# Block products by Strassen's scheme in the second product of two MLPs of a float32 encoder

## The chip, the cores and the metric

One core of a Trainium2 chip runs the whole kernel. The metric is the device time of one execution in microseconds; of several runs the median counts.

## The reference

Four layers with residual adds on x (256 tokens, 1024 features, float32): an attention layer, an MLP, a second attention layer (dilated windows), an MLP, and a last RMSNorm. The change is in the MLPs:

```
def sq_relu_mlp(xn, w1, w2):
    return jnp.square(jax.nn.relu(xn @ w1)) @ w2
...
    x = x + sq_relu_mlp(rms_norm(x, norm_mlp[layer]), mlp_w1[layer], mlp_w2[layer])
```

w1 is 1024 x 4096, w2 is 4096 x 1024.

## The kernel before

Every product is computed with operands split in two: hi (a cast on ScalarE, ACT) and lo (the value less hi, a subtraction on VectorE, DVE), and `mm3` (L170) issues three matmuls, hi by hi, hi by lo and lo by hi. So each weight tile passes through a fixed path. `load_weight` (L129) has SyncE's queue (SP) load a raw tile of 128 x 2048 (1 MB) into one of four buffers; `split_piece` (L144) splits it in four pieces of 512 into whi (L167) and wlo (L168); `weight` (L158) hands it to TensorE (PE) and, before that, loads up to four tiles and splits up to two tiles ahead. The order of the tiles stands in the list `specs`; `plan_mlp` (L104) writes an MLP's part of it: up 0, up 1, up 2, down 0, up 3, down 1 and so on to down 15. Each engine works its queue in order; the scheduler sorts the instructions into it when the program is built, and a block under `tc.high_priority` goes earlier.

An MLP (`mlp`, L308) has 16 steps over 256 hidden features each. `up(j)` (L313) computes two blocks of 128 hidden features for the 256 tokens, 48 matmuls with 256 columns, into one PSUM bank `w`; then relu on ACT (L325), its product with itself `hsq` on DVE (L327), and the split into hh and hl. `down(j)` multiplies the hidden blocks by the w2 tile: two blocks of tokens t, two blocks of hidden features f, two halves of the output features h, that is 2 x 2 x 2 = 8 block products of three matmuls with 512 columns, `mm_down` (L345), all summed in four PSUM banks `acc`, one for each t and h. PE's order is up 0, up 1, up 2, down 0, up 3, down 1 and so on.

`hand_over` (L262) precedes each MLP: from the banks of the layer before, DVE adds into x (L270), two blocks at a time, and `prepare` (L204) makes xh on ACT (L207) and xl on DVE (L208); up 0 takes them in that order, k = 0 to 3 first. The squares of x for the norm follow on DVE (L215, L217).

The first MLP ends in `turn_over` (L360): the last two steps are done bank by bank, and each finished bank is scaled by ACT into y (L390), transposed by PE (L372), added into x by DVE (L374) and made into xh and xl for the next layer, while PE goes on with the next bank; the fourth bank is turned behind the first value products of the next layer. The second MLP ends in `finish` (L394): x has been transposed to tokens first between the steps; each bank is scaled and added by DVE in one instruction (`residual`, L425), the last bank in two parts, then its squares are summed (L455), POOL (GpSimd) raises the sum to the power -1/2 (L198), and ACT and DVE scale the last two blocks, which go out on two queues.

Of the kernel before, what the change touches and what calls it, by code (L numbers as in the profile page):

```python
# [44 lines left out]
def trunk(ctx, tc, a, out):  # L46
# [97 lines left out]
    def split_piece(eng=None):  # L144
        j, i = divmod(state["split"], WPARTS)
        if i == 0:
            parts[j][1:] = (wsp.tile([P, WCH], F32R, tag=n, name=n) for n in ("whi", "wlo"))
        raw, hi, lo = (z[:, cut(j, i, WPARTS)] for z in parts[j])
        state["split"] += 1
        return split(hi, lo, raw, eng)  # L150
# [900 lines left out]
```

## Time and profile before

| | us |
|---|---|
| median of 3 runs | 755.83 (755.81 to 755.87) |
| the profiled execution, its own time | 755.33 |
| its span | 753.6 |
| PE busy | 746.0 (99%) |
| DVE busy | 503.5 (67%) |
| ACT busy | 503.0 (67%) |
| POOL busy | 8.3 (1%) |
| bytes moved by DMA | 129.08 MB, mean 171 GB/s |

The profile is one execution; its lines name the engine, the line of the kernel (L168), the operation and the tiles as out<-in. A matmul's row gives its start and a duration that overlaps with the next one; the distance between two starts is what one costs. "Idle before" is the time in which the engine waited, with what released it.

### The profile page before, as it was taken

Reading aid. Unit: us, or ns where it says so; the run is one execution under the profiler, and the core shown is the slowest. Engines: PE = TensorE matmul, PEld = TensorE weight load, DVE = VectorE, ACT = ScalarE, POOL = GpSimd, SP = SyncE. Lnnn points to the kernel's source line nnn. Section 1 sums busy time; section 2 is a strip of 40 time slices with the busy share of each in tenths; the row PEclk is TensorE's granted clock in tenths of the full one; section 3 lists DMA queues with packets and bytes.
Section 4 is the critical chain, followed back from the end, with each engine's and each line's share of the span. In section 5 each row is a group of like instructions: output and inputs, shape, how many; then the busy total and the mean of one; then the engine's idle time right before and its main releaser. Section 6 shows DMA issues by size and latency. Waiting matters only on the chain.

```text
span 753.6 us, 13848 instructions
## 1 busy us (share of the span) xinstructions
PE 746.0 (99%) x5532; PEld 697.1 (93%) x5532; DVE 503.5 (67%) x1035; ACT 503.0 (67%) x1068; POOL 8.3 (1%) x19
## 2 busy tenths in 40 slices
PE   9999999999999999999999999999999999999996
PEld 6998999899899898999999999999999999899895
DVE  6878858555555556886777677677768554555564
ACT  7778867554554546988988989889856544544541
POOL 0100000000000001000000000000000000000000
PEclk9999999999999999999999999999999999999999
DMA  8772324555455544544453444444553545455501
GB/s 316 278 266 99 114 112 168 177 215 175 180 204 178 187 167 150 209 152 141 168 161 142 159 166 171 156 140 168 205 216 135 195 174 197 173 190 183 187 22 56
DMA packets 22383, 129.08 MB, mean 171 GB/s; under 512 B 2864, under 2 KB 4400, under 8 KB 9648
## 3 DMA queue, kind: packets, MB, share of 16 engines
q1 hardware_dynamic: 22032, 127.94, 47.8%
q8 instruction: 43, 0.70, 0.4%
q10 hardware_dynamic: 288, 0.28, 0.1%
q14 instruction: 20, 0.16, 0.1%
HBM read 127.16 MB, written 1.05 MB: 170 GB/s over the span
## 4 chain that ended last, share of the span: by engine, by line
PE 97%; ACT 1%; issue 1%; DVE 0%; POOLq 0%; POOL 0%
PE acc L171 21%; PE acc L172 20%; PE acc L173 20%; PE w L171 9%; PE w L173 9%; PE w L172 9%; PE w L180 1%; PE w L899 1%; PE w L716 1%; PE w L881 1%; PE acc L914 1%; PE w L730 1%; PE w L622 1%; PE acc L82 0%; PE acc L730 0%
## 5 line engine op out<-in xcount | busy, mean ns | idle before, releaser
L168 DVE TENSOR_TENSOR wlo<-raw,whi 128x512 fp32r<-128x512 f32 (+3 forms) x488 | 307.5, 664 | 168.9 <-ACT whi L167 168.4
L167 ACT CAST whi<-raw 128x512 fp32r<-128x512 f32 (+3 forms) x488 | 268.6, 600 | 190.8 <-issue 167.1
L173 PE MATMUL w<-xh,wlo 128*128 128x256 f32 x528 | 149.4, 283 | 0.0
L172 PE MATMUL w<-xl,whi 128*128 128x256 f32 x528 | 149.4, 283 | 0.0
L171 PE MATMUL w<-xh,whi 128*128 128x256 f32 x528 | 149.4, 283 | 0.0
L171 PE MATMUL acc<-xh,whi 128*128 128x256 f32 x432 | 125.4, 290 | 0.0
L173 PE MATMUL acc<-xh,wlo 128*128 128x256 f32 x432 | 122.3, 283 | 0.0
L172 PE MATMUL acc<-xl,whi 128*128 128x256 f32 x432 | 122.1, 283 | 0.0
L171 PEld LDWEIGHTS w<-xh,whi 128*128 128x128 f32 x528 | 101.3, 192 | 1.1
L172 PEld LDWEIGHTS w<-xl,whi 128*128 128x128 f32 x528 | 101.3, 192 | 1.1
L173 PEld LDWEIGHTS w<-xh,wlo 128*128 128x128 f32 x528 | 101.3, 192 | 0.0
L171 PE MATMUL acc<-whi,hh 128*128 128x512 f32 x250 | 98.1, 392 | 0.0
L172 PE MATMUL acc<-wlo,hh 128*128 128x512 f32 x250 | 97.8, 391 | 0.0
L173 PE MATMUL acc<-whi,hl 128*128 128x512 f32 x250 | 97.5, 390 | 0.0
L171 PEld LDWEIGHTS acc<-xh,whi 128*128 128x128 f32 x432 | 82.6, 191 | 1.3 <-issue 0.3
L172 PEld LDWEIGHTS acc<-xl,whi 128*128 128x128 f32 x432 | 82.7, 191 | 0.0
L173 PEld LDWEIGHTS acc<-xh,wlo 128*128 128x128 f32 x432 | 82.6, 191 | 0.0
L171 PE MATMUL acc<-whi,xh 128*128 128x384 f32 (+2 forms) x160 | 56.0, 350 | 0.0
L173 PEld LDWEIGHTS acc<-whi,hl 128*128 128x128 f32 x250 | 46.9, 188 | 9.8
L171 PEld LDWEIGHTS acc<-whi,hh 128*128 128x128 f32 x250 | 47.0, 188 | 9.1
L172 PEld LDWEIGHTS acc<-wlo,hh 128*128 128x128 f32 x250 | 47.1, 188 | 8.8
L172 PE MATMUL acc<-wlo,xh 128*128 128x384 f32 (+2 forms) x160 | 55.2, 345 | 0.0
(197 smaller groups left out, 1085.1 us busy)
## 6 DMA issues: line engine op xcount, KB each, us to landing
raw<-in_w SPq DMA_DIRECT2D x64, 1024.0 KB, 4.8
raw<-in_w_oqk SPq DMA_DIRECT2D x24, 1024.0 KB, 4.8
raw<-in_w_ov SPq DMA_DIRECT2D x16, 768.0 KB, 4.3
raw<-in_w_oe SPq DMA_DIRECT2D x4, 1024.0 KB, 5.3
raw<-in_w_oo SPq DMA_DIRECT2D x4, 1024.0 KB, 4.8
raw<-in_w_qk SPq DMA_DIRECT2D x3, 1024.0 KB, 9.1
raw<-in_w_cv SPq DMA_DIRECT2D x6, 464.0 KB, 7.8
bias<-in_rpb SPq DMA_DIRECT2D x8, 256.0 KB, 3.4
```

Of the source, the lines that this page charges most:

```text
L167: a = nc.scalar.copy(hi, src).ins
L168: return a, (eng or nc.vector).tensor_tensor(lo, src, hi.bitcast(F32), op=ALU.subtract).ins
L171: nc.tensor.matmul(o, sh, mh, start=first, stop=False)
L172: nc.tensor.matmul(o, sh, ml, start=False, stop=False)
L173: nc.tensor.matmul(o, sl, mh, start=False, stop=last)
L180: nc.tensor.matmul(o[j], y[pb, 0, ts], z[pb, 1, :], start=n == 0, stop=n == 2)
L622: nc.tensor.transpose(pt[0:96, i * P:(i + 1) * P], src[:, i, :], ident)
L716: nc.tensor.transpose(pt[:, b * P:(b + 1) * P], pp[:, b // 2, (b % 2) * P:(b % 2 + 1) * P], ident)
L730: nc.tensor.matmul(pvo[64 * j:64 * j + 64, 0:P], v[:, kk, h * 64:(h + 1) * 64], pts[:, 2 * j + kk, :], start=kk == 0, stop=kk == NT - 1)
L881: nc.tensor.matmul(ss[i, j][rows, T:T + P], d["q12"][:, j, i * P + 64 * c:i * P + 64 * c + 64], d["k12"][:, j, 2 * i + c, :], start=True, ...
L899: nc.tensor.transpose(pt[:, b * P:(b + 1) * P], pp[:, b * P:(b + 1) * P], ident)
L914: nc.tensor.matmul(pvo[cs, tok(i)], d["v0"][:, kk, cs], pts[j][:, kk, :], start=kk == 0, stop=False)
```

## The change

Of each step's second product, the 2 x 2 blocks of hidden values (t by f) and the 2 x 2 blocks of the w2 tile (f by h) are multiplied by seven products in place of eight. Four products (P1, P2, Q3, Q5 on the weight side) take a block as stored or one sum, three take larger sums; each of the seven has a PSUM bank of its own through the whole MLP, so that all eight banks are in use with the one of `up`. The outputs are combined from the seven banks once, at the end of the MLP.

For that:

- The w2 tile is stored as blocks b11, b21, b22, b12. SP loads the 1 MB as before and b12 (256 KB) a second time, into the tile `sum`. Two accumulating transfers from POOL's queue add b11 onto the fourth block of the raw tile and b22 onto the first of `sum`. DVE makes two more sums of 512 columns (`more_sums`, L174 and L175; called S1 and S2 below), and the three blocks of `sum` are split like weights, in one piece of 1536 (sumh, suml). Tiles of `sum`, sumh and suml have two buffers.
- The pieces of all MLP weights' splits are 1024 columns in place of 512.
- Hidden values: relu and the square on ACT, three differences on DVE (L367 to L369), and one split of seven blocks, 896 columns (hh, hl).
- `turn_over` combines the seven banks by instructions of DVE (L400), each a bank times a token's scale (one over the mean square of x) plus or minus a tile; four groups of transposes use the bank of `up`. Two of the four turns (`late`) are done between the next layer's value products, whose order is changed.
- `finish` combines likewise; the 16 transposes of x stand behind the last `up`, and the last product, Q4, is made in two parts of 256 columns.

The lines of the changed kernel are other ones: splits are L196 and L197, the sums into x L299, xh and xl L236 and L237, the sum of the turned block into x L419.

```diff
-        for j in (0, 1):
-            specs.append((a["w1"][layer, j], WCH))
-        for j in range(2, 16):
-            specs.append((a["w1"][layer, j], WCH))
-            specs.append((a["w2"][layer, j - 2], WCH))
-        for j in (14, 15):
-            specs.append((a["w2"][layer, j], WCH))
+        up = [(a["w1"][layer, j], WCH, 2, False) for j in range(16)]
+        down = [(a["w2"][layer, j], WCH, 2, True) for j in range(16)]
+        specs.extend(up[:3])
+        for j in range(13):
+            specs.extend((down[j], up[j + 3]))
+        specs.extend(down[13:])
...
+        if blocks:
+
+            b11, b22, b12 = (src[:, b * BLK:(b + 1) * BLK] for b in (0, 2, 3))
+            sums = state["pool"].tile([P, 3, BLK], F32, tag="sum", name="sum", bufs=2)
+            nc.sync.dma_start(sums[:, 0, :], b12)
+            nc.gpsimd.dma_start(raw[:, 3 * BLK:], b11, accum_op=ALU.add)
+            nc.gpsimd.dma_start(sums[:, 0, :], b22, accum_op=ALU.add)
+            parts[j].append(sums)
...
+                more_sums(*parts[j])
+        if i == n:
+            parts[j][4:] = (state["pool"].tile([P, 3, BLK], F32R, tag=n, name=n, bufs=2) for n in ("sumh", "suml"))
...
+    def more_sums(raw, hi, lo, sums):
+
+        nc.vector.tensor_tensor(sums[:, 1, :], sums[:, 0, :], raw[:, 0:BLK], op=ALU.add)
+        nc.vector.tensor_tensor(sums[:, 2, :], sums[:, 1, :], raw[:, BLK:2 * BLK], op=ALU.add)
...
+    HID = {"Q3": 0, "Q6": 1, "Q5": 2, "Q7": 3, "P2": 4, "Q4": 5, "P1": 6}
+
+
+    COL = {"P1": 0, "P2": 1, "Q3": 2, "Q5": 3, "Q7": 4, "Q6": 5, "Q4": 6}
+    PRODUCTS = ("P1", "P2", "Q5", "Q7", "Q3", "Q6", "Q4")
...
-                        mm3(pu[:, f * T:(f + 1) * T], w[0][:, c], w[1][:, c], xT[0][:, k, :], xT[1][:, k, :],
+                        mm3(pu[:, (1 - f) * T:(2 - f) * T], w[0][:, c], w[1][:, c], xT[0][:, k, :], xT[1][:, k, :],
                             k == 0 and (f == 0 or j > 0), k == KT - 1 and (f == 1 or j > 0))
             r = scratch([512], "relu")
             nc.scalar.activation(r, pu, AF.Relu)
-            h = scratch([512], "hsq")
-            nc.vector.tensor_tensor(h, r, pu, op=ALU.mult)
-            hs[j] = tuple(mp.tile([P, 512], F32R, tag=n, name=n, bufs=4) for n in ("hh", "hl"))
-            split(*hs[j], h)
+            h = mp.tile([P, 8, P], F32, tag="h", name="h", bufs=1)
+            nc.scalar.activation(h[:, 4:8, :], r.rearrange("p (b n) -> p b n", n=P), AF.Square)
+            nc.vector.tensor_tensor(h[:, 2:4, :], h[:, 7:8, :].broadcast_to([P, 2, P]), h[:, 5:7, :], op=ALU.subtract)
+            nc.vector.tensor_tensor(h[:, 1, :], h[:, 6, :], h[:, 2, :], op=ALU.subtract)
+            nc.vector.tensor_tensor(h[:, 0, :], h[:, 4, :], h[:, 1, :], op=ALU.subtract)
+            hh = act.tile([P, KT // 2, T], F32R, tag="quarter", name="hh", bufs=4).rearrange("p a (b n) -> p (a b) n", n=P)
+            hl = mp.tile([P, 7, P], F32R, tag="hl", name="hl", bufs=3)
+            hs[j] = hh, hl
+            split(hh[:, 0:7, :], hl, h[:, 0:7, :])
+
+        def down(j, w, o, n, first, last, c=slice(0, BLK)):
+            i, b = HID[n], COL[n]
+            mm3(o, hs[j][0][:, i, :], hs[j][1][:, i, :], w[0][b][:, c], w[1][b][:, c], first, last)
...
+        m = {n: bank("w" if i < 3 else "acc") for i, n in enumerate(("P1", "P2", "Q6", "Q3", "Q5", "Q7", "Q4"))}
+        pu = bank("w")
+        for j in range(14):
+            if j:
+                up(j + 2, pu)
             w = weight()
-            for f in range(2):
-                down(j, w, f)
-            if j + 3 < 16:
-                up(j + 3)
-            beside(j)
-        return accs, hs, inv, {j: weight() for j in tail}
-
-    def mm_down(acc, hs, j, w, f, t, c0, c1, first, last):
-
-        tk, c = slice(f * T + t * P, f * T + (t + 1) * P), slice(f * D + c0, f * D + c1)
-        mm3(acc, hs[j][0][:, tk], hs[j][1][:, tk], w[0][:, c], w[1][:, c], first, last)
+            for n in PRODUCTS:
+                down(j, w, m[n], n, j == 0, j == 13 and n in apart)
...
+    def onto_tokens(o, m, scale, v, op=ALU.add):
+
+        nc.vector.scalar_tensor_tensor(o, m, scale, v, ALU.mult, op)
...
+        sc = lambda: scratch([512], "y")
+        last("P1")
+        with tc.high_priority(NORM_PRIO):
+            p0, p1 = sc(), sc()
+            nc.scalar.activation(p0, m["P1"], AF.Copy, scale=i0)
+            nc.scalar.activation(p1, m["P1"], AF.Copy, scale=i1)
+        last("P2")
+        y[0, 0] = step(sc(), "P2", i0, p0)
+        last("Q6")
+        v0 = step(sc(), "Q6", i0, p0, ALU.subtract)
+        turn(0, 0)
+        last("Q5")
+        v0 = step(sc(), "Q5", i0, v0)
+        last("Q3")
+        y[0, 1] = step(sc(), "Q3", i0, v0)
+        v1 = step(sc(), "Q6", i1, p1, ALU.subtract)
+        last("Q7")
+        v1 = step(sc(), "Q7", i1, v1)
+        y[1, 1] = step(sc(), "Q5", i1, v1)
+        turn(0, 1)
+        last("Q4")
+        y[1, 0] = step(sc(), "Q4", i1, v1, ALU.subtract)
+        return xT, s, [lambda: turn(1, 1), lambda: turn(1, 0)]
...
+        last("Q3")
+        onto_tokens(v[0, 1], m["Q3"], i0, v[0, 1])
         ss = work.tile([P, 4], F32, tag="ssf", name="ss")
+        for h in range(2):
+            square_sum(v[0, h], ss[:, h:h + 1])
+        w1 = scratch([512], "w1")
+        onto_tokens(w1, m["Q6"], i1, p1, ALU.subtract)
+        onto_tokens(v[1, 1], m["Q5"], i1, v[1, 1])
+        last("Q7")
         nc.vector.tensor_scalar(ss[:, 2:3], ss[:, 0:1], ss[:, 1:2], EPS, ALU.add, ALU.add)
         r = rsqrt(ss[:, 2:3], "x")
         for h, cs in enumerate(HALF):
             y = scratch([512], "y")
+            nc.vector.scalar_tensor_tensor(y, v[0, h], r, g[h], ALU.mult, ALU.mult)
             nc.sync.dma_start(out[0:P, cs], y)
 
 
         ss = work.tile([P, 4], F32, tag="ssf", name="ss")
         xg = [scratch([512], "xg") for _ in range(2)]
...
+        for i, c in enumerate((slice(0, 256), slice(256, 512))):
+            o = bank("w")[:, 0:256]
+            last("Q4", o, c)
+            z = v[1, 0][:, c]
+            onto_tokens(z, o, i1, z)
+            if i == 0:
+                square_sum(z, ss[:, 1:2])
...
-        v0[0]()
-        late()
-        run_all(v0[1:])
+
+        run_all([late[0], v0[0], late[1], v0[1], v0[3], v0[2]])
```

The steady step on DVE. Before, one step of the first MLP (raw, whi, wlo: weights; hsq, hl: hidden values):

```order
L168 TENSOR_TENSOR wlo<-raw,whi 128x512 [waits DMAHW0_49,PE_49,Activation_49]
L327 TENSOR_TENSOR hsq<-relu,w 128x512 [waits Activation_49]
L168 TENSOR_TENSOR wlo<-raw,whi 128x512 [waits Activation_49] x2
L168 TENSOR_TENSOR hl<-hsq,hh 128x512 [waits Activation_49]
L168 TENSOR_TENSOR wlo<-raw,whi 128x512 [waits Activation_49]
L168 TENSOR_TENSOR wlo<-raw,whi 128x512 [waits DMAHW1_49,Activation_49]
L168 TENSOR_TENSOR wlo<-raw,whi 128x512 [waits Activation_49] x3
```

After, one step of it:

```order
L174 TENSOR_TENSOR sum<-sum,raw 128x512 [waits DMAHW4_49,DMASW6_49]
L175 TENSOR_TENSOR sum<-sum,raw 128x512 [waits DVE_49]
L197 TENSOR_TENSOR wlo<-raw,whi 128x1024 [waits PE_49,Activation_49]
L197 TENSOR_TENSOR wlo<-raw,whi 128x1024 [waits DMASW5_49,Activation_49]
L367 TENSOR_TENSOR h<-h 128x256 [waits Activation_49]
L368 TENSOR_TENSOR h<-h 128x128 [waits DVE_49]
L369 TENSOR_TENSOR h<-h 128x128 [waits DVE_49]
L197 TENSOR_TENSOR wlo<-raw,whi 128x1024 [waits DMAHW2_49,Activation_49]
L197 TENSOR_TENSOR wlo<-raw,whi 128x1024 [waits Activation_49]
L197 TENSOR_TENSOR hl<-h,hh 128x896 [waits Activation_49]
L197 TENSOR_TENSOR suml<-sum,sumh 128x1536 [waits Activation_49]
```

Nine subtractions and one product, all of 512, have become eleven instructions of other sizes, and the two sums S1 and S2 (L174, L175), which wait for transfers of SP and of POOL's queue (DMAHW, DMASW), stand between the split of the three sums and the splits of the tile that is due next.

The entry of the second MLP on DVE. Before, from the first sum into x:

```order
L270 TENSOR_TENSOR x<-acc,x 128x512 [waits PE_49] x2
L208 SCALAR_TENSOR_TENSOR xl<-x,gains,xh 128x256 [waits Activation_49] x4
L270 TENSOR_TENSOR x<-acc,x 128x512 [waits PE_49] x2
L168 TENSOR_TENSOR wlo<-raw,whi 128x512 [waits DMAHW0_49,Activation_49]
L208 SCALAR_TENSOR_TENSOR xl<-x,gains,xh 128x256 [waits Activation_49] x4
L215 TENSOR_TENSOR squares<-squares,q 128x512
L215 TENSOR_TENSOR squares<-squares,q 128x512 [waits DVE_49,Activation_49]
```

After, the same place:

```order
L299 TENSOR_TENSOR x<-acc,x 128x512 [waits PE_49] x2
L237 SCALAR_TENSOR_TENSOR xl<-x,gains,xh 128x256 [waits Activation_49] x4
L299 TENSOR_TENSOR x<-acc,x 128x512 [waits PE_49] x2
L174 TENSOR_TENSOR sum<-sum,raw 128x512 [waits DMAHW1_49,DMASW1_49]
L197 TENSOR_TENSOR wlo<-raw,whi 128x1024 [waits DMAHW0_49,Activation_49]
L237 SCALAR_TENSOR_TENSOR xl<-x,gains,xh 128x256 [waits Activation_49] x4
L244 TENSOR_TENSOR squares<-squares,q 128x512
L197 TENSOR_TENSOR wlo<-raw,whi 128x1024 [waits Activation_49]
L244 TENSOR_TENSOR squares<-squares,q 128x512 [waits DVE_49]
L175 TENSOR_TENSOR sum<-sum,raw 128x512
```

Between the second pair of sums into x and the second four xl, where one split of 512 stood, there are now S1 of the first down tile, with its waits for two transfers, and a split of 1024.

The end of the first MLP on DVE. Before, from the first sum of a turned block into x (y is combined output, xl and wlo belong to the next layer):

```order
L374 TENSOR_TENSOR x<-w,x 128x4x128 [waits PE_49]
L208 SCALAR_TENSOR_TENSOR xl<-x,gains,xh 128x128 [waits Activation_49] x4
L374 TENSOR_TENSOR x<-w,x 128x4x128 [waits PE_49]
L208 SCALAR_TENSOR_TENSOR xl<-x,gains,xh 128x128 [waits Activation_49] x4
L374 TENSOR_TENSOR x<-w,x 128x4x128 [waits PE_49]
L168 TENSOR_TENSOR wlo<-raw,whi 128x384 [waits DMAHW0_49,Activation_49]
L208 SCALAR_TENSOR_TENSOR xl<-x,gains,xh 128x128 [waits Activation_49] x4
L168 TENSOR_TENSOR wlo<-raw,whi 128x384 [waits Activation_49]
L374 TENSOR_TENSOR x<-w,x 128x4x128 [waits PE_49]
L168 TENSOR_TENSOR wlo<-raw,whi 128x384 [waits Activation_49] x2
L208 SCALAR_TENSOR_TENSOR xl<-x,gains,xh 128x128 [waits Activation_49] x4
```

After, from the first combination:

```order
L400 SCALAR_TENSOR_TENSOR y<-w,ms,y 128x512 [waits PE_49,Activation_49]
L400 SCALAR_TENSOR_TENSOR y<-w,ms,y 128x512 [waits PE_49]
L197 TENSOR_TENSOR wlo<-raw,whi 128x384 [waits DMAHW0_49,Activation_49]
L419 TENSOR_TENSOR x<-w,x 128x4x128 [waits PE_49]
L400 SCALAR_TENSOR_TENSOR y<-acc,ms,y 128x512 [waits DVE_49]
L197 TENSOR_TENSOR wlo<-raw,whi 128x384 [waits Activation_49]
L237 SCALAR_TENSOR_TENSOR xl<-x,gains,xh 128x128 [waits Activation_49] x3
L400 SCALAR_TENSOR_TENSOR y<-acc,ms,y 128x512 [waits DVE_49]
L237 SCALAR_TENSOR_TENSOR xl<-x,gains,xh 128x128 [waits Activation_49]
L400 SCALAR_TENSOR_TENSOR y<-w,ms,y 128x512
L419 TENSOR_TENSOR x<-w,x 128x4x128 [waits PE_49]
L400 SCALAR_TENSOR_TENSOR y<-acc,ms,y 128x512 [waits DVE_49]
```

The scaling of the finished banks, which stood on ACT, has become combinations on DVE (L400), in one queue with the sums into x, the xl and the next layer's first splits.

More of the change, by code (lines that the diff above doesn't have):

```diff
@@ L38 @@
 RAWBUFS = 4
+BLK = 512
 LOAD_AHEAD = 4
@@ L144, in split_piece @@
     def split_piece(eng=None):
-        j, i = divmod(state["split"], WPARTS)
+        j, i = state["split"]
+        _, _, n, blocks = specs[j]
+        state["split"] = (j, i + 1) if i < n - (not blocks) else (j + 1, 0)
         if i == 0:
[L147 to L150, printed above, removed]
+            parts[j][1:3] = (wsp.tile([P, WCH], F32R, tag=n, name=n) for n in ("whi", "wlo"))
+            if blocks:
+                more_sums(*parts[j])
+        if i == n:
+            parts[j][4:] = (state["pool"].tile([P, 3, BLK], F32R, tag=n, name=n, bufs=2) for n in ("sumh", "suml"))
+            sums, hi, lo = parts[j][3:]
+        else:
+            raw, hi, lo = parts[j][:3]
+            raw, hi, lo = (z[:, cut(j, i, n)] for z in (raw, hi, lo))
+            return split(hi, lo, raw, eng)
+        return split(hi, lo, sums)
+    def more_sums(raw, hi, lo, sums):
+        nc.vector.tensor_tensor(sums[:, 1, :], sums[:, 0, :], raw[:, 0:BLK], op=ALU.add)
+        nc.vector.tensor_tensor(sums[:, 2, :], sums[:, 1, :], raw[:, BLK:2 * BLK], op=ALU.add)
     def prefetch(loads, splits):
@@ L163, in weight @@
         state["used"] = j + 1
-        return parts.pop(j)[1:]
+        raw, hi, lo, *sums = parts.pop(j)
+        if sums:
+            blocks = lambda z, n: [z[:, b * BLK:(b + 1) * BLK] for b in range(n)]
+            return [blocks(z, 4) + [t[:, b, :] for b in range(3)] for z, t in ((hi, sums[1]), (lo, sums[2]))]
+        return hi, lo
     def split(hi, lo, src, eng=None):
@@ new lines, in mlp, with last @@
+        inv = inverse_columns(s)
+        m = {n: bank("w" if i < 3 else "acc") for i, n in enumerate(("P1", "P2", "Q6", "Q3", "Q5", "Q7", "Q4"))}
[3 more added lines that the diff above has]
+                up(j + 2, pu)
+            w = weight()
+            for n in PRODUCTS:
+                down(j, w, m[n], n, j == 0, j == 13 and n in apart)
+        tail = {j: weight() for j in (14, 15)}
+        def last(n, o=None, c=slice(0, BLK)):
+            for j, w in tail.items():
+                down(j, w, m[n] if o is None else o, n, o is not None and j == 14, j == 15, c)
@@ L398, in finish @@
-        nc.sync.dma_start(g, a["norm_final"].partition_broadcast(P))
-        xt = mp.tile([P, NT, D], F32, name="xt")
-        tail = range(13, 16)
-        def down(accs, hs):
-            def step(j, w, f):
-                for i in range(4):
-                    end = tail[0] - 1 if i == 3 else 15
-                    mm_down(accs[i], hs, j, w, f, i // 2, (i % 2) * 512, (i % 2) * 512 + 512, (j, f) == (0, 0), (j, f) == (end, 1))
-            return step
-        def tokens_first(j):
-            if j % 2 == 0 and j < 8:
-                t, h = j // 4, j // 2 % 2
-                pt = bank("w")
-                for k in range(4):
-                    nc.tensor.transpose(pt[:, k * P:(k + 1) * P], x[:, 4 * h + k, tok(t)], ident)
-                nc.scalar.copy(xt[:, t, HALF[h]], pt)
@@ L430, in finish @@
[L430 to L433 removed]
+        m, last, inv, pu = mlp(mp, xT, s, ("Q4",))
+        i0, i1 = (column(inv, t) for t in range(NT))
+        xt = half_tile(act, "xt", 2).bitcast(F32).rearrange("p k n -> p (k n)").rearrange("p (t d) -> p t d", t=NT)
+        g = [scratch([512], "gain") for _ in HALF]
+        for h, cs in enumerate(HALF):
+            nc.sync.dma_start(g[h], a["norm_final"][cs].partition_broadcast(P))
@@ new lines, in finish, with square_sum @@
+        for t in range(NT):
+            for h, cs in enumerate(HALF):
+                for k in range(4):
+                    nc.tensor.transpose(pu[:, k * P:(k + 1) * P], x[:, 4 * h + k, tok(t)], ident)
+                nc.scalar.copy(xt[:, t, cs], pu)
+        v = {(t, h): xt[:, t, HALF[h]] for t in range(NT) for h in range(2)}
+        def square_sum(z, o):
+            nc.scalar.activation(scratch([z.shape[-1]], "junk"), z, AF.Square, scale=D ** -0.5, accum_out=o)
+        last("P1")
+        p0, p1 = scratch([512], "p0"), scratch([512], "p1")
@@ L808, in gemm @@
                     wt.append(weight())
-                if half == 0:
+                first = i not in acc
+                if first:
                     acc[i] = bank("acc")
```

121 lines of the change are left out of this document (49 added, 72 removed).

## Prediction

> **What bounds the kernel now.** I read the page's table of engines and its chain of waits first: they ask whether removing TensorE work can shorten the run at all.
>
> ```profile
> PE 746.0 (99%) x5532; PEld 697.1 (93%) x5532; DVE 503.5 (67%) x1035; ACT 503.0 (67%) x1068; POOL 8.3 (1%) x19
> PE 97%; ACT 1%; issue 1%; DVE 0%; POOLq 0%; POOL 0%
> ```
>
> TensorE is busy for 746.0 of 753.6 us and is 97% of the chain, so a matmul that goes is worth its time, as long as nothing else becomes late. Next comes the table of stretches, for the steady part of the first MLP (columns: window, length, then busy time of PE, weight loads, DVE, ACT, POOL, the granted clock, DMA share, GB/s), and the timeline of one step in it: first two matmuls of a down product, the first of the up product, the first of the next down product.
>
> ```profile
> 137.00:287.00 150.00, 150.00 (x956) 136.83 (x955) 82.53 (x134) 71.61 (x134) 0.00 (x0) 1.00 0.53 185
> 200.20 0.40 PE L171 MATMUL acc<-whi,hh 128*128 128x512 f32 x1
> 200.44 0.40 PE L172 MATMUL acc<-wlo,hh 128*128 128x512 f32 x1
> 205.67 0.28 PE L171 MATMUL w<-xh,whi 128*128 128x256 f32 x1
> 211.42 0.40 PE L171 MATMUL acc<-whi,hh 128*128 128x512 f32 x1
> ```
>
> The clock is 1.00 and PE has no gap. Down: 205.67 - 200.20 = 5.47 us for 24 matmuls of 512 columns, 0.228 each. Up: 5.75 us for 48 of 256, 0.120 each. A step is 11.22 us, and the window's DVE share is 55%, ACT's 48%, the DMA engines' 53%.
>
> **What goes.** Seven block products of three matmuls replace eight: 21 per step for 24. Over 16 steps and two MLPs that is 96 x 0.228 = 21.9 us; I use 21.8. The new step is 10.54 us.
>
> **What is added per step.** The durations come from the groups of instructions (busy time, mean ns of one).
>
> ```profile
> L168 DVE TENSOR_TENSOR wlo<-raw,whi 128x512 fp32r<-128x512 f32 x400 | 261.0, 686 | 156.2 <-ACT whi L167 155.9
> L217 DVE TENSOR_TENSOR squares<-squares 128x256 f32<-128x256 f32 x4 | 1.7, 420 | 0.0
> L168 DVE TENSOR_TENSOR obl<-w,obh 128x128 fp32r<-128x128 f32 x8 | 2.3, 288 | 4.5 <-ACT obh L167 4.5
> L167 ACT CAST whi<-raw 128x512 fp32r<-128x512 f32 x400 | 227.6, 619 | 182.1 <-issue 163.1 <-PE acc L173 10.3 <-PE acc L172 5.4
> L167 ACT CAST whi<-raw 128x384 fp32r<-128x384 f32 x68 | 31.2, 509 | 4.7 <-issue 2.4 <-PE acc L172 1.0 <-ACT xh L207 1.0
> L325 ACT ACTIVATE relu<-w 128x512 f32<-128x512 f32 x32 | 19.0, 593 | 0.0
> ```
>
> DVE costs (686 - 420) / 256 = 1.04 ns an element and 0.15 us an instruction; by that 1024 elements take 1.22 us, 1536 take 1.75, 896 take 1.08. A step before has ten DVE instructions of 0.69, 6.9 us. After, it has four splits of 1024 (4.88), one of 1536 (1.75), one of 896 (1.08), the two block sums S1 and S2 (1.37) and three differences of the hidden blocks (0.42 + 2 x 0.29): 10.1 us apart, about 9.6 back to back. That is 91 to 96% of 10.54. ACT, at 0.86 ns an element, has 4 x 1.06 + 1.50 + 0.95 + 0.59 + 0.62 = 7.9 us. So DVE fits, with under 1 us to spare, and the splits run two tiles ahead of TensorE, which hides jitter. I cost the steady step at nothing beyond its matmuls; without that cover every 0.1 us of DVE over 10.54 costs 26 x 0.1 = 2.6 us (13 alternating steps in each MLP).
>
> DMA traffic per step rises from 2 MB to 2.75 MB. No accumulating transfer and none from GpSimd's queue stands in the trace before, so I bound them by these rows (KB each, us to landing):
>
> ```profile
> raw<-in_w SPq DMA_DIRECT2D x64, 1024.0 KB, 4.8
> raw<-in_w_qk SPq DMA_DIRECT2D x3, 1024.0 KB, 9.1
> bias<-in_rpb SPq DMA_DIRECT2D x8, 256.0 KB, 3.4
> out<-y SPq DMA_DIRECT2D x2, 256.0 KB, 2.1
> ```
>
> A 256 KB accumulate thus costs between 2.1 (the lone store) and 9.1 us (a load in the crowded start); I take 3.4, the row of its size beside other loads. The DMA share becomes 0.53 x 2.75/2 x 11.22/10.54 = 0.78 if accumulates cost like loads, 0.92 if double. The loop to watch: a down tile's raw buffer is reloaded once DVE has split it, and S1 of that new tile stands on DVE ahead of the next tile's two splits, which free the next buffer. Landing + S1 + S2 + two splits = landing + 4.0 us with gaps must fit in 10.54, so landing may be up to 6.5 us; it is 4.8 now, and with 256 KB of accumulate beside each 1 MB I estimate 4.8 x 1.25 = 6.0. For the small tile (its 256 KB load, then the accumulate) two steps are there, 21.1 us less about 9.6 of DVE rows and 3.4 for the load: an accumulate of up to 8 us fits.
>
> [...]
>
> **The second MLP's entry.** S1 of the first down tile stands on DVE between the residual sums and the second four xl (lo parts of x), on which up 0's matmuls of k = 4 to 7 wait. Timelines of before, SP's queue, DVE and PE:
>
> ```profile
> 561.04 0.33 SPq L136 DMA_DIRECT2D raw<-in_w  x1
> 565.21 1.28 DVE L270 TENSOR_TENSOR x<-acc,x 128x512 f32<-128x512 f32 x2
> 567.01 1.67 DVE L208 SCALAR_TENSOR_TENSOR xl<-x,gains,xh 128x256 fp32r<-128x256 f32 x4
> 565.26 0.28 PE L171 MATMUL w<-xh,whi 128*128 128x256 f32 x1
> ```
>
> Up 0 starts at 565.26, and k = 4 comes after 24 matmuls, at 568.14. On SP the new 256 KB load stands behind the load of 561.04, so it is issued at 561.4 and lands at about 566.6 (behind 1 MB that lands at 565.8). Its accumulate lands 3.4 later, at 570.1. Then S1 (0.62), the 1024 split (1.2) and the first xl (0.42): 572.3, a stall of 4.2 us. Ends: 1.0 (load alone 3.4, accumulate 2.1) and 9.8 (9.1). Behind the wait are the xl, the squares and the splits of up 1; all slip with PE.
>
> **The first MLP's entry.** The same rows stand there, but the block is asked for far earlier (up 3's raw load, ahead of it on SP, is at 103.50 and the residual sums at 114.83), so only S1 and the longer split stand in the way: 566.5 + 0.6 + 1.2 + 0.4 on the clock above is 568.7 for 568.14. I take 0.5, between 0 and 1.
>
> ```profile
> 103.50 0.33 SPq L136 DMA_DIRECT2D raw<-in_w  x1
> ...
> 114.83 1.28 DVE L270 TENSOR_TENSOR x<-acc,x 128x512 f32<-128x512 f32 x2
> ```
>
> **The end of the first MLP.** Before, each token-and-half needs one scaled copy on ACT. After, DVE combines products: 7 instructions like the second row here, and all x sums, xl and first weight splits of the next layer stand in the same queue.
>
> ```profile
> L374 DVE TENSOR_TENSOR x<-w,x 128x512 f32<-128x512 f32 x4 | 2.8, 690 | 2.7 <-PE w L372 2.6
> L425 DVE SCALAR_TENSOR_TENSOR xt<-acc,ms,xt 128x512 f32<-128x512 f32 x4 | 2.9, 751 | 4.7 <-PE acc L173 4.7
> 289.73 1.23 DVE L208 SCALAR_TENSOR_TENSOR xl<-x,gains,xh 128x128 fp32r<-128x128 f32 x4 [0.47 <-ACT xh L207]
> 299.35 1.02 DVE L168 TENSOR_TENSOR wlo<-raw,whi 128x384 fp32r<-128x384 f32 x2
> 297.89 0.66 PE L372 MATMUL w<-ident,y 128*128 128x128 f32 x4
> 298.30 0.42 PE L171 MATMUL acc<-whi,xh 128*128 128x384 f32 x1
> 298.91 0.33 PE L171 MATMUL acc<-whi,xh 128*128 128x384 f32 x1
> 300.99 0.33 PE L171 MATMUL acc<-whi,xh 128*128 128x384 f32 x1
> ```
>
> From the end of product P2, DVE has 7 x 0.75 + 4 x 0.69 + 16 x 0.30 + 4 x 0.50 + 0.6 = 15.4 us to the last xl, and 0.4 for hand-overs (xl and wlo at the back-to-back pitch of the third and fourth row, 1.23 / 4 and 1.02 / 2). PE has 19 matmuls of 512 (4.3), four groups of transposes at 298.30 - 297.89 = 0.41 (1.6) and 38 of 384 columns at (300.99 - 298.91) / 12 = 0.173 (6.6): 12.5. The difference, 3.3 us, is PE's stall; ends 0 (were the next layer's order to hide it) and 6 (if the hi splits that ACT does ahead of the last hidden tile delay that as well).
>
> **The end of the program.** Timeline of before:
>
> ```profile
> 747.13 0.28 PE L173 MATMUL w<-whi,hl 128*128 128x256 f32 x1
> 747.97 0.48 DVE L455 CUSTOM_DVE_ANT_0 junk<-xt,ss 128x256 f32<-128x256 f32 x1
> 748.54 0.67 POOL L198 TENSOR_TENSOR rstd<-ss,mhalf 128x1 f32<-128x1 f32 x1 [7.09 <-DVE ss L455]
> 749.24 0.72 ACT L461 ACTIVATE xg<-xg,rstd 128x512 f32<-128x512 f32 x1 [2.92 <-POOL rstd L198]
> ```
>
> The program ends 6.2 us after its last matmul (747.41 to 753.6), 5.15 after the DVE sum of squares. After, that sum stands at the end of a longer queue: from the end of product Q3, DVE has six combinations (4.5), three 512 sums or products (2.1), four of 256 (1.8), the sum of squares (0.6), two small ones (0.4) and about 0.9 of waits for ACT, less 0.8 of pitch: 9.5. PE has 18 matmuls left, 6 x 0.228 + 12 x 0.12 = 2.8. So the end is 9.5 + 5.15 - 2.8 = 11.8 us behind the last matmul, 5.5 more than before; ends 4 and 6.5. The 16 transposes of x only move from between the steps to the end.
>
> **Sum.** -21.8 + 0.5 + 3.3 + 4.2 + 5.5 = -8.3. The profiled execution took 755.33 us (span 753.6 and 1.7 around it), 0.5 below the median of 755.83. 755.33 - 8.3 = 747.0; on the median's scale 747.5. The case's own range, from the ends: 739 to 757.
>
> **Rivals.**
> *Loads become the bound (slower).* If a landing, slowed by reading and writing back in the accumulates, takes over 6.5 us, each step grows by the excess; at 6.9 the whole 8.3 us is gone (26 x 0.32), at 7.5 the step is 11.5 and the time 773. The page's DMA row bears on it, in tenths for 40 slices of the span:
>
> ```profile
> DMA  8772324555455544544453444444553545455501
> ```
>
> For: in the first slice, at a share of 0.8 to 0.9, 1 MB took the 9.1 us above, and a share of 0.78 to 0.92 is estimated here. Against: the start's loads are issued all at once, these spaced. [...]
> *DVE becomes the bound.* If hand-overs with ACT make its 10.1 us into 10.85, 26 x 0.3 = 8 us are lost: 755.
> *The gain stays whole.* If the accumulate lands early and the ends overlap as their lower ends say, 739 or a little less.
> That the products are not removed is excluded: the order of PE has 5156 matmul rows for 5264.
>
> **Chances.** Forecast 0.52, loads 0.22, DVE 0.13, whole gain 0.13. Faster by over 0.2% (1.5 us, about what a measurement of this kernel can tell): forecast nearly whole, whole gain, a quarter of DVE's: 0.66. Within 0.2%: 0.07. Slower: 0.27. The range of 739 to 768 takes in the forecast's bounds, DVE's case and landings up to 7.3 us; left out are a few in a hundred below and the worse landings above.
>
> **What would show it.** In the trace after: PE's steady step of 10.54 us without waits, and DVE busy over 90% there; a wait of PE on xl of 4.2 us in the second MLP's entry and none above 1 in the first; waits of about 3.3 us among the transposes at the first MLP's end; 11.8 us from the last matmul to the end. Wrong would be a step over 10.8 us with PE waiting for wlo or suml, raw landings above 6.5 us, or DVE's S1 waiting each step.

## The result and the profile after

The changed kernel took 816.56 us (median of 4 runs, 814.86 to 818.15) for 755.82 before: 1.080 times as long, interval 1.078 to 1.083. The forecast was 747.5, within 739 to 768. Its profiled execution took 815.58 us, with a span of 813.8.

The page of the changed kernel: the engines' busy time, the granted clock in tenths and the DMA share by slices, the chain that ended last, and the DMA issues.

```profile
PE 753.0 (93%) x5424; PEld 692.3 (85%) x5424; DVE 615.9 (76%) x1084; ACT 560.7 (69%) x1003; POOL 64.2 (8%) x83
...
PEclk9999999999899998999999999999999998899977
DMA  8662468585788975453453453444667667699921
...
DMA 11%; DVE 8%; issue 4%; ACT 2%; PE 1%; POOL 0%; POOLq 0%; DVEq 0%; ACTq 0%; SPq 0%
...
raw<-in_w SPq DMA_DIRECT2D x64, 1024.0 KB, 5.7
...
raw<-in_w POOLq DMA_DIRECT2D x32, 256.0 KB, 6.2
sum<-in_w SPq DMA_DIRECT2D x32, 256.0 KB, 4.9
sum<-in_w POOLq DMA_DIRECT2D x32, 256.0 KB, 6.9
```

Three sums come out of the first row and that of before. TensorE is idle for 813.8 - 753.0 = 60.8 us where it was 7.6: 53.2 more. It is busy for 753.0 us although 21.8 us of matmuls went from 746.0: 28.8 more, at a mean granted clock of 0.962 for 0.998. So 53.2 + 28.8 - 21.8 = 60.2, the growth of the span. The chain, 97% PE before, can be followed back for only 26% of the span now, the second MLP, and leads through transfers and VectorE there. The accumulates (the rows POOLq) take 6.2 and 6.9 us to landing.

What VectorE waited for, from the list of waits (us in total, times, longest):

```profile
DVE sum L174 <- DMA sum<-in_w: 82.2, 27, 6.3
...
DVE sum L174 <- DMA raw<-in_w: 7.2, 2, 3.6
```

S1 (L174), the instruction that adds the first weight block to the accumulated sum, waits in 27 of 32 tiles for the accumulate into `sum`. The raw loads are late twice.

From one relu to the next, the steps 3 to 15 of the first MLP, in us:

| | steps |
|---|---|
| before | 11.7, then 11.2 throughout |
| after | 14.3 15.9 11.8 15.0 18.4 10.3 13.3 10.6 10.9 11.6 11.4 10.7 18.3 |

The second MLP reads 14.6 13.4 11.9 14.8 18.1 10.3 12.9 and then about 10.5 to 11.5, with 15.0 at its end. So most of the later steps run nearly at the 10.54 us of the forecast, and the early ones do not. The last step of each MLP is long as well; in the first MLP, S1 (at 294.48) waits 5.2 us there for an accumulate that takes 9.4 us to land. The timelines of SP, POOL and DVE show why. First an early stretch of the second MLP, from the load of b12 into a free buffer of `sum` on:

```profile
626.72 0.33 SPq L145 DMA_DIRECT2D sum<-in_w  x1
...
630.52 0.86 POOL L147 DMA_DIRECT2D sum<-in_w  x1 [2.35 <-DVE h L368]
...
637.25 0.69 DVE L174 TENSOR_TENSOR sum<-sum,raw 128x512 f32<-128x512 f32 x1 [3.79 <-DMA sum<-in_w]
639.00 1.75 DVE L197 TENSOR_TENSOR suml<-sum,sumh 128x1536 fp32r<-128x1536 f32 x1
640.78 0.33 SPq L145 DMA_DIRECT2D sum<-in_w  x1
...
645.45 0.86 POOL L147 DMA_DIRECT2D sum<-in_w  x1
...
652.90 0.69 DVE L174 TENSOR_TENSOR sum<-sum,raw 128x512 f32<-128x512 f32 x1 [4.14 <-DMA sum<-in_w]
```

A buffer comes free when suml has been split; at once b12 is loaded into it, then b22 is accumulated, then S1 may run, 640.78 to 652.90, 12.1 us. And in this stretch S1 of a tile stands ahead of the suml of the tile before. So the ring of two buffers turns once for each step: S1, suml, load, accumulate, next S1, 15.6 us here. In the regular steps further on, S1 stands behind that suml, and each buffer has two steps for its turn:

```profile
726.53 0.33 SPq L145 DMA_DIRECT2D sum<-in_w  x1
...
731.54 0.86 POOL L147 DMA_DIRECT2D sum<-in_w  x1 [4.17 <-DVE h L367]
...
738.25 0.69 DVE L174 TENSOR_TENSOR sum<-sum,raw 128x512 f32<-128x512 f32 x1 [1.23 <-DMA sum<-in_w]
```

11.7 us for load and accumulate and some 9.6 of VectorE's rows from S1 to suml make 21.3, for two steps of 10.54, 21.1: it is at its limit, and S1 waits a little in each step.

### The profile page after: what moved, and what is told of

The parts are those of the page before. It is cut to its first block, busy times and chain, and to the rows that moved or that the text cites. A ratio compares the mean times of both kernels' runs of the same rounds, so it can differ in the third digit from the quotient of the medians.

```text
span 813.8 us, 13992 instructions
## 1 busy us (share of the span) xinstructions
PE 753.0 (93%) x5424; PEld 692.3 (85%) x5424; DVE 615.9 (76%) x1084; ACT 560.7 (69%) x1003; POOL 64.2 (8%) x83
## 3 DMA queue, kind: packets, MB, share of 16 engines
q0 software_dynamic: 9216, 16.78, 12.9%
## 5 line engine op out<-in xcount | busy, mean ns | idle before, releaser
L197 DVE TENSOR_TENSOR wlo<-raw,whi 128x512 fp32r<-128x512 f32 (+3 forms) x360 | 294.6, 843 | 35.3 <-ACT whi L196 34.7
L196 ACT CAST whi<-raw 128x512 fp32r<-128x512 f32 (+3 forms) x360 | 252.9, 744 | 31.3 <-PE acc L202 11.0
L200 PE MATMUL w<-xh,whi 128*128 128x256 f32 x528 | 154.6, 293 | 15.5 <-ACT relu L364 15.4
L201 PE MATMUL w<-xl,whi 128*128 128x256 f32 x528 | 153.4, 291 | 3.1 <-DVE xl L237 3.1
L200 PEld LDWEIGHTS w<-xh,whi 128*128 128x128 f32 x528 | 105.2, 199 | 22.1 <-ACT relu L364 21.3
L196 ACT CAST hh<-h 128x896 fp32r<-128x896 f32 x32 | 30.2, 943 | 127.6 <-DVE h L369 127.6
L174 DVE TENSOR_TENSOR sum<-sum,raw 128x512 f32<-128x512 f32 x32 | 22.1, 691 | 89.4 <-DMA sum<-in_w 82.2
L146 POOL DMA_DIRECT2D raw<-in_w x32 | 28.1, 877 | 490.0 <-issue 245.3
L196 ACT CAST sumh<-sum 128x1536 fp32r<-128x1536 f32 x32 | 47.2, 1475 | 14.8 <-DVE sum L175 14.8
L197 DVE TENSOR_TENSOR suml<-sum,sumh 128x1536 fp32r<-128x1536 f32 x32 | 56.0, 1750 | 0.3 <-ACT sumh L196 0.3
L202 PE MATMUL acc<-whi,xl 128*128 128x384 f32 (+2 forms) x160 | 54.8, 343 | 0.0
```

Of the source, the lines that this page charges most:

```text
L146: nc.gpsimd.dma_start(raw[:, 3 * BLK:], b11, accum_op=ALU.add)
L174: nc.vector.tensor_tensor(sums[:, 1, :], sums[:, 0, :], raw[:, 0:BLK], op=ALU.add)
L196: a = nc.scalar.copy(hi, src).ins
L197: return a, (eng or nc.vector).tensor_tensor(lo, src, hi.bitcast(F32), op=ALU.subtract).ins
L200: nc.tensor.matmul(o, sh, mh, start=first, stop=False)
L201: nc.tensor.matmul(o, sh, ml, start=False, stop=False)
```

## The experiments

Theory A: the ring of the small tile (its load, the slow accumulate, S1 ahead of suml, two buffers) holds up VectorE, and it TensorE. The rivals: VectorE is too full, or the 16 DMA engines are. Times of single runs stand beside a run of the kernel before on the same chip (755.57 to 755.72).

**Three buffers of the small tile.**

```diff
-            sums = state["pool"].tile([P, 3, BLK], F32, tag="sum", name="sum", bufs=2)
+            sums = state["pool"].tile([P, 3, BLK], F32, tag="sum", name="sum", bufs=3)
```

> The changed kernel with three buffers of the small tile sum in place of two, nothing else. Theory A (the ring of the small tile: a buffer comes free when suml is done, then the 256 KB load of 4.9 us, then the accumulate of 6.5 us, then S1 on VectorE, which in the early steps stands ahead of the next suml): a third buffer gives that chain one more step of 10.5 us, the waits of S1 nearly go, and the time falls from 816 to 760 or less. Theory B (VectorE itself is too full, or the 16 DMA engines are): the buffer changes nothing, 805 or more.

Measured: 755.02 us in one run, 61.5 below the changed kernel, by a change of one number in it. The engines and S1's waits:

```profile
PE 729.9 (97%) x5424; PEld 679.7 (90%) x5424; DVE 615.5 (82%) x1084; ACT 562.6 (75%) x1003; POOL 64.1 (9%) x83
```

```profile
DVE sum L174 <- DMA raw<-in_w: 21.2, 15, 2.7
DVE sum L174 <- DMA sum<-in_w: 11.5, 4, 3.3
```

VectorE does the same 615 us of work, and the transfers are no faster (accumulates 5.4 and 7.4, raw loads 6.9 us); only the ring is longer, and the waits for `sum` fall from 82.2 to 11.5, while those for raw loads rise from 7.2 to 21.2. Theory A stands, both rivals fall as the main cause.

**Plain loads in place of the accumulates** (two block sums are left out).

```diff
-            nc.gpsimd.dma_start(raw[:, 3 * BLK:], b11, accum_op=ALU.add)
-            nc.gpsimd.dma_start(sums[:, 0, :], b22, accum_op=ALU.add)
+            nc.gpsimd.dma_start(raw[:, 3 * BLK:], b11)
+            nc.gpsimd.dma_start(sums[:, 0, :], b22)
```

> The two accumulating transfers of each down tile become plain loads of the same bytes from the same queue (the sums of the blocks are left out, the output is another one). Theory A1 (it is the accumulating itself that takes 6.5 us): the transfers land in about 3.4 us, the loop of 14.3 us in the early steps becomes about 11.2, and the time falls to 775 to 790. Theory A2 (it is GpSimd's queue or the shared DMA engines that make a transfer take 6.5 us, whatever it does): they still land in 6 us or more, and the time stays above 805.

Measured: 782.11 us in one run, with landings of

```profile
raw<-in_w POOLq DMA_DIRECT2D x32, 256.0 KB, 4.8
sum<-in_w SPq DMA_DIRECT2D x32, 256.0 KB, 4.4
sum<-in_w POOLq DMA_DIRECT2D x32, 256.0 KB, 5.5
```

The time is in A1's range, the landings are in neither's: of the 6.9 us, 1.4 go with the accumulating, the rest stays with plain loads. The early steps follow the ring. Its terms (load, second transfer, S1, suml) are 4.4 + 5.5 + 0.7 + 1.75 = 12.4 us here and 4.9 + 6.9 + 0.7 + 1.75 = 14.3 in the changed kernel; the steps 3 to 6 of the first MLP take 12.5 and 14.2 in the mean.

**No accumulates** (two block sums are missing).

```diff
-            nc.gpsimd.dma_start(raw[:, 3 * BLK:], b11, accum_op=ALU.add)
-            nc.gpsimd.dma_start(sums[:, 0, :], b22, accum_op=ALU.add)
```

> The two accumulating transfers of each down tile are left out (two of the block sums are missing, the output is another one); the load of b12, the sums on VectorE and all splits stay. Theory A: S1 waits only for the loads, the steps go back to about 10.5 us, and the time is 740 to 752, with the ends of both MLPs as they are. Theory B (VectorE is the bound with 10.1 us of work in a step): steps of 11 us or more remain, 770 or more.

Measured: 740.88 us in one run, steps of 10.5 from the seventh on, TensorE 98% busy, and a load of b12 that lands in 3.4 us:

```profile
PE 725.2 (98%) x5424; PEld 677.7 (92%) x5424; DVE 616.7 (83%) x1084; ACT 562.3 (76%) x1003; POOL 8.2 (1%) x19
...
sum<-in_w SPq DMA_DIRECT2D x32, 256.0 KB, 3.4
```

The forecast without its accumulates, 747.5 less the 4.2 us of the second entry, is 743.3, and the run is 2.4 below that. VectorE with the same work as in the changed kernel does not bind.

**The sums on GpSimd.** All four are its own adds out of the raw tile.

```diff
-            b11, b22, b12 = (src[:, b * BLK:(b + 1) * BLK] for b in (0, 2, 3))
...
-            nc.sync.dma_start(sums[:, 0, :], b12)
-            nc.gpsimd.dma_start(raw[:, 3 * BLK:], b11, accum_op=ALU.add)
-            nc.gpsimd.dma_start(sums[:, 0, :], b22, accum_op=ALU.add)
+            blk = lambda b: raw[:, b * BLK:(b + 1) * BLK]
+            for o, u, v in ((sums[:, 0, :], blk(3), blk(2)), (sums[:, 1, :], sums[:, 0, :], blk(0)),
+                            (sums[:, 2, :], sums[:, 1, :], blk(1)), (blk(3), blk(3), blk(0))):
+                nc.gpsimd.tensor_tensor(o, u, v, op=ALU.add)
...
-            if blocks:
-                more_sums(*parts[j])
```

> All four block sums of a down tile are made by GpSimd's own adds out of the raw tile (no second load of b12, no accumulating transfer, no S1 and S2 on VectorE). Theory A: no transfer stands in the chain, VectorE has 8.7 us in a step, and if an add of 512 columns takes GpSimd at most 2 us the time is 735 to 752. If VectorE and GpSimd hold each other up (both read two tiles of SBUF), VectorE's instructions get longer and the time is 760 or more.

Measured: 813.68 us in one run, with steps of 12.5. Groups of it (busy time, mean ns of one):

```profile
L195 DVE TENSOR_TENSOR wlo<-raw,whi 128x1024 fp32r<-128x1024 f32 x128 | 209.7, 1671 | 6.5 <-ACT whi L194 6.4
L195 DVE TENSOR_TENSOR suml<-sum,sumh 128x1536 fp32r<-128x1536 f32 x32 | 69.1, 2161 | 0.3 <-ACT sumh L194 0.3
```

```profile
L147 POOL TENSOR_TENSOR sum<-sum,raw 128x512 f32<-128x512 f32 x64 | 126.1, 1970 | 2.5
```

A split of 1024, 1217 ns in the changed kernel, takes 1671 in the mean where GpSimd adds, and VectorE becomes the bound: its nine instructions of a step take 12.6 us in the mean (4 x 1.67 + 2.16 + 1.52 + 0.86 + 0.75 + 0.61), as long as the step. The second branch of the expectation came true.

**S1 and S2 behind the splits of their tile** (e5 in the expectations), two buffers as in the changed kernel.

```diff
-            if blocks:
-                more_sums(*parts[j])
         if i == n:
+            with tc.issue_after(state["last"]):
+                more_sums(*parts[j])
...
-            return split(hi, lo, raw, eng)
+            done = split(hi, lo, raw, eng)
+            state["last"] = done[1]
+            return done
```

> The changed kernel with S1 and S2 of a down tile queued on VectorE behind the splits of that tile in place of ahead of them; two buffers of sum as before, the same transfers and the same work. Theory A (the ring of the small tile, closed within one step where S1 stands ahead of the next suml): the ring now has about 14 us from suml to the S1 of the tile that takes its buffer, for 12 us of load and accumulate; the steps go to 10.5 us and S1 no longer stands ahead of the xl at the entries: 740 to 752. Rival (the accumulates are too slow for two buffers wherever S1 stands, only a third buffer helps): 780 or more. Rival (VectorE too full): no less than 800.

Measured: 761.34 us (756.79 to 766.36, 8 runs), 1.0065 of before, interval 1.0034 to 1.0096. It lies 9 above the forecast's 740 to 752 and below what either rival gave. The order alone brings 55 of the 61 us that the changed kernel lost. The transfers are slower than in the changed kernel, and S1 still waits:

```profile
sum<-in_w SPq DMA_DIRECT2D x32, 256.0 KB, 6.0
sum<-in_w POOLq DMA_DIRECT2D x32, 256.0 KB, 7.7
...
DVE sum L176 <- DMA sum<-in_w: 32.2, 18, 3.8
```

So the ring of two steps is again at its limit.

**Both cures**, the order of the last one and three buffers.

> Both: S1 and S2 behind the splits of their tile, and three buffers of sum. Theory A: one cure is enough, so the time is that of e5 within 2 us, and 5 to 12 below that of three buffers alone (755), since the wait of the xl at the second MLP's entry goes. If the accumulates also slow the raw loads (DMA engines full), it stays at 750 or above.

Measured: 744.59 us in one run, 16.7 below the order alone and 10.4 below the buffers alone: each cure leaves something to the other. The distance to the buffers alone was forecast as 5 to 12; that the order alone would give the same time was wrong. Of the 17 us to the order alone, 10 lie at the ends of the two MLPs: from the last relu of one to the first of the other it takes 295.4 us for 302.6, and 27.7 for 31.0 behind the last relu. All steps take 10.54 us from the fourth on, and S1 (L176 there) no longer waits:

```profile
L176 DVE TENSOR_TENSOR sum<-sum,raw 128x512 f32<-128x512 f32 x32 | 22.0, 687 | 0.0
```

The accumulates take 8.1 us there and the raw loads 7.2, and it costs nothing: the DMA engines' fullness is not the bound.

**One accumulate** (e7 in the expectations). VectorE makes b12 + b22 out of the raw tile; the accumulate into the raw tile stays.

```diff
-            nc.sync.dma_start(sums[:, 0, :], b12)
+            nc.vector.tensor_tensor(sums[:, 0, :], raw[:, 3 * BLK:], raw[:, 2 * BLK:3 * BLK], op=ALU.add)
             nc.gpsimd.dma_start(raw[:, 3 * BLK:], b11, accum_op=ALU.add)
-            nc.gpsimd.dma_start(sums[:, 0, :], b22, accum_op=ALU.add)
```

> b12 + b22 is made by VectorE out of the raw tile: no second load of b12 and no accumulate into sum; the accumulate into the raw tile's fourth block stays, off the chain of S1. VectorE gets a twelfth instruction of 0.69 us, 10.8 us a step apart and about 10.2 back to back, for TensorE's 10.54. Theory A: no transfer but the raw load stands ahead of S1, the waits on sum go, and the time is 742 to 755, by how far VectorE's extra 0.69 us shows. If VectorE at over 10.5 us is what costs, the steps are 11 us or more and the time is 760 or more.

Measured: 743.31 us in one run. VectorE's twelfth instruction does not show in the steps, most of them of 10.54 us, and the accumulate lands in 4.2 us. The same kernel was timed again:

> The kernel of e7 once more, timed against the kernel before in five rounds: a single run gave 743.31 for 755.57. If that holds, 742.5 to 744.5, a ratio of 0.983 to 0.985 with an interval that leaves out 1. If the single run was a lucky one, 746 to 752.

Measured: 744.72 us (743.98 to 745.34, 5 runs), 0.985 of before, interval 0.984 to 0.986; 0.2 above the range that I gave, and 1.5% faster than the kernel before.

**All sums on VectorE.**

```diff
-            b11, b22, b12 = (src[:, b * BLK:(b + 1) * BLK] for b in (0, 2, 3))
...
-            nc.sync.dma_start(sums[:, 0, :], b12)
-            nc.gpsimd.dma_start(raw[:, 3 * BLK:], b11, accum_op=ALU.add)
-            nc.gpsimd.dma_start(sums[:, 0, :], b22, accum_op=ALU.add)
+            blk = lambda b: raw[:, b * BLK:(b + 1) * BLK]
+            nc.vector.tensor_tensor(sums[:, 0, :], blk(3), blk(2), op=ALU.add)
+            nc.vector.tensor_tensor(blk(3), blk(3), blk(0), op=ALU.add)
```

> All four block sums of a down tile on VectorE out of the raw tile: no transfer from GpSimd's queue at all, no second load. VectorE has 13 instructions a step, 11.5 us apart and about 10.8 back to back, for TensorE's 10.54. Theory A (transfers, not VectorE, made the changed kernel slow): steps of 10.6 to 11.2, the time 745 to 762. Rival (VectorE's share was what the changed kernel failed on): with 1.4 us more on VectorE than the changed kernel has, it is no better than that one, 800 or more.

Measured: 749.74 us in one run, within the forecast. A stretch of its first MLP (length, then busy time of PE, weight loads, DVE, ACT and POOL):

```profile
160.00:280.00 120.00, 119.92 (x776) 109.58 (x775) 120.00 (x151) 83.57 (x95) 0.00 (x0) 1.00 0.53 195
```

VectorE is busy without a gap for 120 us, and TensorE still hardly waits: 11.5 us of instructions apart go into 10.54. What it loses to the one-accumulate kernel lies at the ends: from the last relu of one MLP to the first of the other 299.4 for 294.4 us, and 29.1 for 26.7 after the last relu.

**The price of an accumulate** in the kernel before: one of 256 KB for each down tile into a tile that nobody reads.

```diff
...
+        if any(src is z for z in downs):
+            nc.gpsimd.dma_start(state["idle"], src[:, 0:512], accum_op=ALU.add)
...
+        state["idle"] = mp.tile([P, 512], F32, name="idle_sum")
+        nc.gpsimd.memset(state["idle"], 0.0)
```

> The kernel before with one accumulating transfer of 256 KB for each down tile from GpSimd's queue into a tile that nobody reads (16 in each MLP, one after the other). It prices the transfer in the DMA traffic of before. If the accumulating itself makes it slow, it takes 5.5 us or more from issue to landing here too; if it is the traffic of the changed kernel, 3 to 4 us. The time stays within 1 us of 755.6 in both, since nothing waits for it.

Measured: 755.81 us in one run, as before, and

```profile
idle_sum<-in_w POOLq DMA_DIRECT2D x32, 256.0 KB, 5.2
```

5.2 us lie between the two branches. With as many bytes in all (137.5 MB), the plain load of this size took 3.4 in the run without accumulates, on SP's queue, and the accumulate of the one-accumulate kernel 4.2. So I put a part of the 6.9 us down to the accumulating (5.5 with plain loads) and a part to the fuller DMA engines of the changed kernel (154.3 MB); how much is whose was not separated.

**The end of the program**, on the one-accumulate kernel: the scaled blocks of the first tokens go behind the last sum of squares.

```diff
-        for h, cs in enumerate(HALF):
-            y = scratch([512], "y")
-            nc.vector.scalar_tensor_tensor(y, v[0, h], r, g[h], ALU.mult, ALU.mult)
-            nc.sync.dma_start(out[0:P, cs], y)
...
+        def out_y(h, cs):
+            with tc.issue_after(done):
+                y = scratch([512], "y")
+                nc.vector.scalar_tensor_tensor(y, v[0, h], r0, g[h], ALU.mult, ALU.mult)
+            nc.sync.dma_start(out[0:P, cs], y)
+
+        out_y(0, HALF[0])
+        done = nc.vector.tensor_scalar(xg[1], xg[1], r, None, ALU.mult).ins
+        out_y(1, HALF[1])
```

> The kernel of e7 (one accumulate, the sum b12 + b22 on VectorE), and at the end of the program the two scaled blocks of the first tokens go behind the second tokens' sum of squares on VectorE, one while GpSimd raises to the power, one last. The chain at the end is on VectorE, so 1.5 us of it leave and 0.5 to 1 come back: 741.5 to 743, 0.5 to 1.5 below e7, and 1.6 to 1.9% below the kernel before.

Measured: 744.76 us (743.9 to 745.53, 4 runs): no gain over 744.72, and 1.8 above the range that I gave. The last part of its SP queue:

```profile
737.42 0.34 SPq L530 DMA_DIRECT2D out<-xg  x1
738.08 0.33 SPq L525 DMA_DIRECT2D out<-y  x1
```

The last block now leaves at 738.08 and the span ends at 742.0. Counted from where VectorE gets the last product that it waits 1.1 us for (727.41; 726.68 in the one-accumulate run), the last sum of squares starts after 7.9 us where it was 9.2, but the last store is issued after 10.7 where it was 11.1, and the span ends after 14.6 where it was 14.7. So the store that was put last takes back most of what VectorE's chain gained.

## Why the prediction was wrong, point by point

- *The matmuls that go, 21.8 us, and the step of 10.54*: right; steps of 10.5 wherever S1 does not wait.
- *VectorE's durations* (1.22, 1.75 and 1.08 us by an element's 1.04 ns) were right, and VectorE was not the bound, as forecast:

```profile
L197 DVE TENSOR_TENSOR wlo<-raw,whi 128x1024 fp32r<-128x1024 f32 x128 | 152.9, 1217 | 7.8 <-ACT whi L196 7.6
L197 DVE TENSOR_TENSOR suml<-sum,sumh 128x1536 fp32r<-128x1536 f32 x32 | 56.0, 1750 | 0.3 <-ACT sumh L196 0.3
L197 DVE TENSOR_TENSOR hl<-h,hh 128x896 fp32r<-128x896 f32 x32 | 34.7, 1085 | 2.0 <-ACT hh L196 2.0
```

- *"I take 3.4, the row of its size beside other loads"*: mis-sized; 6.9 us, and 4.9 for the load of b12 that I also put at 3.4. Both lie within the bounds of 2.1 and 9.1, but I carried those bounds only into the entry's stall and not into the steps, although the upper one is above the 8 us that I said would fit. The lowest median for an accumulate of 256 KB in any run is 4.2 us, with one accumulate for each tile, and 5.2 were measured beside the transfers of before.
- *"For the small tile ... two steps are there ... an accumulate of up to 8 us fits"*: this is the step that failed. I read it off a regular step of VectorE's order. In the first steps of each MLP the order puts S1 ahead of the suml of the tile before, and the ring turns once a step: 4.9 of load, 0.7 of S1 and 1.75 of suml leave 3.2 of 10.54 us for an accumulate of 6.9. With my 3.4 us for both transfers this ring would have taken 9.3 us and have fitted, so the whole loss needed both errors; but a look at those steps would have put the limit at 10.54 - 3.4 - 0.7 - 1.75 = 4.7 us, within the bounds, and the rival's chance far above 22%. The runs with three buffers (755.02) and with S1 behind its splits (761.34) each take most of the loss away, and with both (744.59) the time is 3 below the forecast of 747.5: the rest of the sum held within a few us.
- *The slower rival* was the right kind, a transfer that bounds the step, in the wrong loop. It watched the raw loads with a limit of 6.5 us; they land in 5.7 in the changed kernel, and in 7.2 in the run with both cures, which keeps its steps of 10.54, so that limit was too low. Its sum at 6.9 was off as well: 26 x 0.4 is 10.4, not 8.3. Of the signs of being wrong that I had named, two came true: steps over 10.8 us in which TensorE waits for wlo and suml (7.7 and 5.3 us in the down products' rows), and S1's waits (27 of 32 tiles).
- *The splits ahead of TensorE as cover*: they did not hide a ring that turned too slowly in each of several steps (14.3, 15.9, 11.8, 15.0 and 18.4 us in the steps 3 to 7 of the first MLP, for 10.54).
- *The clock*: my sum had no term for it. Windows of 2 us of the changed kernel, around a wait of 3.8 us (busy time of PE, weight loads, DVE, ACT, POOL, then the granted clock):

```profile
686.00:688.00 2.00, 1.31 (x6) 0.75 (x4) 2.00 (x3) 0.36 (x1) 0.00 (x0) 1.00 1.04 301
688.00:690.00 2.00, 0.00 (x0) 0.00 (x0) 0.09 (x1) 1.83 (x2) 0.00 (x0) 1.00 0.96 369
690.00:692.00 2.00, 0.87 (x4) 0.87 (x5) 0.31 (x1) 2.00 (x4) 0.00 (x0) 0.50 0.87 369
694.00:696.00 2.00, 2.00 (x12) 2.00 (x11) 2.00 (x3) 1.80 (x2) 0.00 (x0) 0.50 0.81 141
696.00:698.00 2.00, 2.00 (x15) 2.00 (x15) 2.00 (x4) 0.00 (x0) 0.00 (x0) 0.79 0.34 114
```

  The wait ends at 691.1; the granted clock is 0.50 from 690 to 696.8 us, so TensorE works at half its clock for 5.7 us, and by that I estimate that the wait of 3.8 costs about 3 us more, half of 5.7. Over the program this is the 28.8 us above, a third of the loss of 82 (53.2 + 28.8); in the run without accumulates TensorE hardly waits, the granted clock is 0.996, and its busy time of 725.2 us is the 746.0 of before less 21.8, and 1.0 more. How long the half clock lasts differs: after the wait of 3.1 us that ends at 601.6 it lasts from 601.2 to 604.7, and after one of 2.7 us that ends at 164.4 from 164.3 to 167.7. So after waits of 3.8, 3.1 and 2.7 us TensorE worked at half clock for 5.7, 3.1 and 3.3 us; no run shows what sets these times.
- *The second MLP's entry, 4.2 us*: the place and the kind of the wait were as described, the size came out near by luck. The load of b12 was issued 10.2 us ahead of the second residual sums (584.57 for 594.74), where I had 3.8 (561.4 for 565.21), but it took 6.6 us to land and the accumulate 7.4, where I had 5.2 and 3.4:

```profile
591.83 1.75 POOL L147 DMA_DIRECT2D sum<-in_w  x2 [5.56 <-PE acc L202]
...
599.29 0.69 DVE L174 TENSOR_TENSOR sum<-sum,raw 128x512 f32<-128x512 f32 x1 [3.27 <-DMA sum<-in_w]
...
601.03 1.66 DVE L237 SCALAR_TENSOR_TENSOR xl<-x,gains,xh 128x256 fp32r<-128x256 f32 x4
```

  TensorE waited 3.1 us for the xl, and then ran at half clock. The first entry, 0.5 by forecast: the second relu comes 0.5 us later than before (127.80 for 127.31).
- *The first MLP's end, 3.3 us*: among the transposes TensorE waited 1.5 us in the changed kernel, 1.4 without accumulates and 3.1 with both cures, so about as forecast at most. *The end of the program, 11.8 us behind the last matmul*: 813.8 less 803.2 (the end of the matmul of 802.94) is 10.6, within the ends that I gave.

## What to carry to other kernels

A ring of buffers is costed as a loop: everything from the buffer's release to its next release, over as many steps as the order really gives it, and the order is read in the first steps of a loop as well as in the regular ones. A transfer of a kind that the trace does not show enters each loop that it closes with its upper bound, not its middle one. Where TensorE sets the time and begins to wait, its slower clock after the waits (28.8 of the 82 us lost here) belongs into the sum.
